# A fused attention and retention layer: keys and values summed in two parts of the model axis, with the sums of the first part kept in DRAM

## The chip, the cores and the metric

The kernel runs on one core of one Trainium2 chip. The metric is device time in microseconds (us) from start to end of one execution. Three runs of the kernel before took 2622.92, 2627.49 and 2629.21 us; the median is 2627.49 us.

## The reference: what is computed

One layer of a diffusion backbone in 32-bit floats: 256 latent tokens and 256 context tokens, model width 4096.

```python
mod = silu(c) @ ada_w + ada_b                   # 4096 x 12288: shift, scale, gate
shift, scale, gate = split(mod, 3)
mod_c = silu(c_ctx) @ ada_w[:, :2*D] + ada_b[:2*D]
h  = rms_norm(x, norm_w) * (1 + scale) + shift
hc = rms_norm(ctx, norm_w) * (1 + scale_c) + shift_c
proj = h @ w_in                                 # 4096 x 14336: q, k, v, gate of both groups
pc   = hc @ w_in[:, keys and values]            # context rows need keys and values only
o_d = diff_attention(...)                       # group A: 8 heads, two softmax maps each
o_r = retention forward + backward              # group B: 8 heads
y = concat(o_d * silu(dg), o_r * silu(rg)) @ w_out   # 4096 x 4096
out = x + gate * y
```

The model axis (4096) is the axis that the projections sum over; it falls into 32 k-tiles of 128. No k-tile of `h` exists before the shift and scale of its 128 columns, and each of these columns is a sum over all 4096 rows of `ada_w`.

## The kernel before, in words

**Exact products.** Every weight k-tile is split into two parts that one pass of the array carries exactly: ScalarE casts the high part (`whi`, L337), VectorE subtracts to get the low part (`wlo`, L338). `h` is held as `hh` and `hl` in SBUF for the whole kernel. One product is three matmuls (hh by hi, hh by lo, hl by hi; L351 to L353, in the startup L489 to L491). A unit is two k-tiles of one head's weights: 512 columns for a head of group A, 384 for one of group B. Keys and values (kv) have four row tiles, latent and context, so a kv unit has 24 matmuls; queries and gate (qg) have two row tiles, so 12. A unit's weights come by SP's queue into `raw` (three buffers); `whi` and `wlo` have four buffers each, which is two units.

**Startup.** `CHUNKS` cuts the model axis into two chunks of one k-tile and fifteen of two. For each chunk the adaLN columns come first: `Ada.unit` (L238) multiplies loaded k-tiles of `ada_w` by the two columns of `c` and `c_ctx` on TensorE, four k-tiles at once in the four column groups of the array (tile `pa`, L253), four loads per call for a chunk of two k-tiles. At the end of a chunk `finish` transposes the sums by small matmuls (`pm`, L268) and VectorE and ScalarE modulate the chunk's k-tiles of `h` in place (L272 to L286). Then the kv units of five heads of group A (A0 to A4) run over the chunk. Heads A0 to A3 take one PSUM bank at a time and add into SBUF on VectorE (`kvqgA`, L497); A4 stays in four banks (`psP`) through the whole startup. `ada_to` places the adaLN bursts among these units, 0.3 of a chunk ahead (`LEAD`).

**Steady state.** `SCHED` orders qg of A0 to A7, kv of A5 to A7, and kv and qg of group B, each over all 32 k-tiles with the sums in PSUM. Between units run steps of the attention of a finished head (`attA`, L614, and `attB`, L722) and, in the kv phases from A6 on, one step of `gate_task` (L804): it loads two k-tiles of the gate columns (`graw`, 512 KB, one load ahead) and VectorE multiplies and adds them into `gacc` (L827, two per step, 128 steps in all). The big SBUF pool `a4` has nine buffers of 4 KB per partition for kv and qg of heads, `graw`, `gacc` and others.

**Output.** The heads' outputs go through DRAM (`o_dram`) and the output projection (`psO`) follows.

The order on each engine is not the program's text: the builder schedules the whole program once against its own estimate of durations, an instruction that is ready going ahead of one that is not, and writes a fixed order for every engine. On the chip each engine works through its order and waits where an operand is late.

Of the kernel before, what the change touches and what calls it, by code (L numbers as in the profile page):

```python
# [10 lines left out]
F32 = mybir.dt.float32  # L11
# [25 lines left out]
CHUNKS = [1, 1] + [2] * 15  # L37
LEAD = 0.3
NS = 5
ADAB = 5  # L40
RAWB = 3

SCHED = ["qg A0", "qg A1", "keep", "kv A5", "qg A2", "qg A3", "gate", "kv A6", "qg A4", "kv A7", "qg A5", "kv B0", "qg A6",
         "kv B1", "qg A7", "kv B2", "attB", "qg B0", "kv B3", "qg B1", "kv B4", "qg B2", "kv B5", "qg B3", "kv B6", "qg B4",
         "kv B7", "qg B5", "qg B6"]
# [27 lines left out]
def hybrid_kernel(es, tc, x, c, ctx, c_ctx, norm_w, ada_w, ada_b, w_in, q_norm_w, k_norm_w,  # L73
# [19 lines left out]

    def aux_tile(shape, name):
        return aux.tile(shape, F32, name=name, tag="aux")
# [5 lines left out]
    tab = cpool.tile([P, C_END], F32, name="tab")  # L101
    nc.scalar.dma_start(tab[:, 0:C_J], ctab[:, 0:C_J])
    ident = tab[:, C_ID:C_ID + P]
    J = tab[:, C_J:C_J + 384]
    cosp = tab[:, C_COS:C_COS + 256].rearrange("p (r d) -> p r d", r=2)
    sinp = tab[:, C_SIN:C_SIN + 256].rearrange("p (r d) -> p r d", r=2)
# [5 lines left out]
    subln = cpool.tile([P, DV], F32, name="subln")  # L112
    retnw = cpool.tile([P, DV], F32, name="retnw")
# [90 lines left out]
    c0s = [sum(CHUNKS[:j]) for j in range(len(CHUNKS))]  # L204
# [6 lines left out]
    ada_end = [sum(1 for a in ada_units if a[0] <= j) for j in range(len(CHUNKS))]  # L211

    class Ada:
# [5 lines left out]
        def load(self):  # L219
            """start the loads of the next unit"""  # L220
# [4 lines left out]
            n = CHUNKS[j] * P  # L225
            c0 = c0s[j] * P
            tiles = []
            # shift and scale columns side by side
            m = 4 // CHUNKS[j]
# [770 lines left out]
```

## Time and profile before

| | before |
|---|---|
| median of 3 runs | 2627.49 us |
| span of the profiled execution | 2625.2 us |
| granted TensorE clock, mean | 0.995 |
| PE busy | 2563.4 us (98%) |
| PEld (weight load) busy | 2114.3 us (81%) |
| VectorE busy | 1550.8 us (59%) |
| ScalarE busy | 990.8 us (38%) |
| read from HBM, written | 523.49 MB, 8.40 MB |

The result does not hold a time of its own for the profiled execution; its span is 2625.2 us, from the first to the last instruction, and it lies among the three runs. The startup lasts from the first projection matmul at 50.0 us to the last one at 680.6 us, the steady state to 2251.3 us, and the output projection to the end. Matmuls are pipelined, so a row's duration (0.40 us for 512 columns) is longer than the distance from one start to the next (0.23 us); a busy PE with fewer instructions per stretch is a slower PE.

### The profile page before, as it was taken

To read this page: it belongs to the slowest core of one execution; us is meant where nothing else is said; L and a number is where in the kernel's file an instruction comes from. 1 tells how busy PE (TensorE), PEld (TensorE's weight loads), DVE (VectorE), ACT (ScalarE), POOL (GpSimd) and SP (SyncE) were. 2 spreads that over 40 slices of the span, in tenths; PEclk is the share of its full clock that TensorE was granted. 3 is DMA by queue.
4 is the path that set the end of the run, shared out by engine and by line. 5 is a ranking of instruction groups with operands and counts; after the bars stand their busy time and mean duration, and the time that the engine had idled before them with its cause. 6 is when DMAs were issued, how large, how long until landed. Compare 5 with 4: busy or idle time off the path is not lost.

```text
span 2625.2 us, 36854 instructions
## 1 busy us (share of the span) xinstructions
PE 2563.4 (98%) x12970; PEld 2114.3 (81%) x12970; DVE 1550.8 (59%) x2898; ACT 990.8 (38%) x1993; POOL 47.3 (2%) x49
## 2 busy tenths in 40 slices
PE   7899999999999999999999999999999999999999
PEld 5466666666778888787989899999999999878887
DVE  6555555555665465756666666657564446755554
ACT  5222222222454453434334433343343445544443
POOL 0000000000000000000000000000000000000000
PEclk8999999999999999999999999999999999999999
DMA  9989988987542453746474757656562546776765
GB/s 308 317 268 291 289 288 276 295 282 222 151 153 93 142 168 120 233 138 211 144 228 150 225 155 208 201 169 219 172 214 89 145 125 189 221 231 206 224 212 173
DMA packets 510521, 534.38 MB, mean 204 GB/s; under 512 B 30640, under 2 KB 433392, under 8 KB 510336
## 3 DMA queue, kind: packets, MB, share of 16 engines
q1 hardware_dynamic: 498176, 511.85, 62.9%
q10 hardware_dynamic: 12160, 20.17, 2.3%
q8 instruction: 103, 1.69, 0.3%
q14 instruction: 82, 0.67, 0.1%
HBM read 523.49 MB, written 8.40 MB: 203 GB/s over the span
## 4 chain that ended last, share of the span: by engine, by line
PE 81%; DMA 11%; DVE 5%; issue 1%; ACT 1%; SPq 1%; POOL 0%; ACTq 0%; DVEq 0%; POOLq 0%
PE psA L352 7%; PE psA L353 7%; PE psA L351 7%; PE psB L352 7%; PE psB L353 7%; PE psB L351 7%; DMA graw<-in_ada_w_dram 6%; PE psO L351 4%; PE psO L352 4%; PE psO L353 4%; PE pa L253 4%; DVE gacc L827 2%; DMA ada<-in_ada_w_dram 2%; PE psA3s L489 1%; PE psA2s L489 1%; PE psA1s L489 1%
## 5 line engine op out<-in xcount | busy, mean ns | idle before, releaser
L352 PE MATMUL psB<-wloB,hh 128*128 128x384 f32 x1536 | 520.8, 339 | 9.4 <-DVE wloB L338 9.3
L353 PE MATMUL psB<-whiB,hl 128*128 128x384 f32 x1536 | 518.0, 337 | 0.0
L351 PE MATMUL psB<-whiB,hh 128*128 128x384 f32 x1536 | 472.3, 338 | 2.0 <-ACT whiB L337 2.0
L338 DVE TENSOR_TENSOR wloB<-rawB,whiB 128x384 fp32r<-128x384 f32 x512 | 280.9, 555 | 242.8 <-ACT whiB L337 241.1
L337 ACT CAST whiB<-rawB 128x384 fp32r<-128x384 f32 x512 | 258.1, 512 | 434.7 <-PE psB L353 371.3
L352 PE MATMUL psA<-wloA,hh 128*128 128x512 f32 x896 | 358.0, 400 | 6.0 <-DVE wloA L338 6.0
L353 PE MATMUL psA<-whiA,hl 128*128 128x512 f32 x896 | 356.1, 397 | 0.0
L338 DVE TENSOR_TENSOR wloA<-rawA,whiA 128x512 fp32r<-128x512 f32 x352 | 241.4, 690 | 193.1 <-ACT whiA L337 191.8
L337 ACT CAST whiA<-rawA 128x512 fp32r<-128x512 f32 x352 | 216.2, 620 | 299.3 <-PE psA L353 251.3
L351 PE MATMUL psA<-whiA,hh 128*128 128x512 f32 x896 | 315.7, 399 | 0.2 <-ACT kvqgA L408 0.2
L352 PEld LDWEIGHTS psB<-wloB,hh 128*128 128x128 f32 x1536 | 289.5, 188 | 16.1 <-DVE wloB L338 14.5
L353 PEld LDWEIGHTS psB<-whiB,hl 128*128 128x128 f32 x1536 | 289.4, 188 | 0.3
L351 PEld LDWEIGHTS psB<-whiB,hh 128*128 128x128 f32 x1536 | 284.5, 188 | 4.4 <-ACT whiB L337 2.6
L338 DVE TENSOR_TENSOR wloO<-rawO,whiO 128x512 fp32r<-128x512 f32 x256 | 175.9, 691 | 150.7 <-ACT whiO L337 150.4
L337 ACT CAST whiO<-rawO 128x512 fp32r<-128x512 f32 x256 | 157.7, 620 | 194.8 <-PE psO L353 165.1
L827 DVE SCALAR_TENSOR_TENSOR gacc<-graw,cT,gacc 128x512 f32<-128x512 f32 x248 | 185.6, 748 | 69.8 <-DMA graw<-in_ada_w_dram 68.2
L352 PEld LDWEIGHTS psA<-wloA,hh 128*128 128x128 f32 x896 | 169.0, 189 | 48.4 <-DVE wloA L338 9.5
L352 PE MATMUL psO<-wloO,ohh 128*128 128x512 f32 x512 | 203.9, 398 | 0.0
L353 PE MATMUL psO<-whiO,ohl 128*128 128x512 f32 x512 | 202.8, 396 | 0.0
L351 PEld LDWEIGHTS psA<-whiA,hh 128*128 128x128 f32 x896 | 168.7, 189 | 40.8 <-ACT kvqgA L408 0.6
L353 PEld LDWEIGHTS psA<-whiA,hl 128*128 128x128 f32 x896 | 169.1, 189 | 39.3
L351 PE MATMUL psO<-whiO,ohh 128*128 128x512 f32 x512 | 162.1, 397 | 1.1 <-ACT whiO L337 0.9
(313 smaller groups left out, 3244.2 us busy)
## 6 DMA issues: line engine op xcount, KB each, us to landing
ada<-in_ada_w_dram SPq DMA_DIRECT2D x512, 256.0 KB
rawA<-in_w_in_dram SPq DMA_DIRECT2D x352, 256.0 KB
graw<-in_ada_w_dram SPq DMA_DIRECT2D x128, 512.0 KB
rawB<-in_w_in_dram SPq DMA_DIRECT2D x256, 256.0 KB
rawO<-in_w_out_dram SPq DMA_DIRECT2D x128, 512.0 KB
rawB<-in_w_in_dram SPq DMA_DIRECT2D x256, 128.0 KB
rawA0s<-in_w_in_dram SPq DMA_DIRECT2D x30, 256.0 KB
rawA1s<-in_w_in_dram SPq DMA_DIRECT2D x30, 256.0 KB
```

What stands on the lines that cost most here:

```text
L253: m = nc.tensor.matmul(self.pa[32 * g:32 * (g + 1), :], cpad[:, 2 * kt:2 * kt + 32], tiles[k], start=(kt < 4), stop=(kt >= KT - 4), tile_p ...
L337: nc.scalar.copy(hi, raw[:, k])
L338: nc.vector.tensor_tensor(lo, raw[:, k], hi.bitcast(F32), op=ALU.subtract)
L351: nc.tensor.matmul(pt[:, :ncol], a, hi, start=f, stop=False)
L352: nc.tensor.matmul(pt[:, :ncol], a, lo, start=False, stop=False)
L353: nc.tensor.matmul(pt[:, :ncol], b, hi, start=False, stop=e)
L489: nc.tensor.matmul(pt, a, hi, start=f, stop=False)
L827: nc.vector.scalar_tensor_tensor(acc, raw[:, k], cT[:, 0, kt:kt + 1], acc, op0=ALU.mult, op1=ALU.add)
```

## The change

The model axis is cut at k-tile 20 (`K1`). The startup now covers k-tiles 0 to 19 alone: two chunks of one and nine of two, with the same five heads. Its adaLN calls take eight k-tiles each, so the bursts on TensorE have eight products (`ADAB`, the buffers for `ada_w`, goes from 5 to 6). At its end the sums of the five heads' keys and values are stored to `p_dram` in DRAM. Then a new phase runs over `FIRST`, the kv units of A5 to A7 and B0 to B7, also over k-tiles 0 to 19; each head's four banks are copied by ScalarE and stored by ScalarE's queue. Between these units `ada2_task` makes the shift and scale of the last 12 k-tiles, in three chunks of four, on VectorE: per k-tile of the sum axis one 512 KB load and two multiply-adds of 128x1024 into two accumulators, then 16 small matmuls against a column of ones per chunk, and the same modulation. The steady state then runs kv over k-tiles 20 to 31 and qg over all 32 for one head after the other; at the third of the six kv units the stored sums are loaded by SP's queue, and VectorE adds PSUM to them. The gate takes two steps per unit in kv of group A and one in kv of group B. The constants of the heads move to a pool that opens when the adaLN pool closes.

```diff
+K1 = 20
+CHUNKS = [1, 1] + [2] * 9
+CHUNKS2 = [4, 4, 4]
-ADAB = 5
+ADAB = 6
+FIRST = [f"A{h}" for h in range(NS, 8)] + [f"B{h}" for h in range(8)]
+SCHED = []
+for _h in range(8):
+    SCHED += [f"kv A{_h}", f"qg A{_h}"]
+SCHED += ["kv B0", "attB", "qg B0"]
...
-        nk = 8 // cn
+        nk = 8
...
+    def ada2_task():
+        work = [(j, k) for j in range(len(CHUNKS2)) for k in range(KT)]
...
+        for i, (j, k) in enumerate(work):
...
+            if k == 0:
+                acc = [a4.tile([P, 2 * n], F32, name=f"acc{j}_{v}", tag="a4") for v in range(2)]
+            for v in range(2):
+                cv = cT[:, v, k:k + 1]
+                if k == 0:
+                    nc.vector.tensor_scalar(acc[v], w, cv, None, op0=ALU.mult)
+                else:
+                    nc.vector.scalar_tensor_tensor(acc[v], w, cv, acc[v], op0=ALU.mult, op1=ALU.add)
+            load()
+            if k == KT - 1:
+                yield
+                pm = aux_tile([P, cn, 4], f"pm2_{j}")
...
+                modulate(c0s2[j], cn, pm)
+            yield
...
+        def before():
+            for i in range(2):
+                hd.dst(2 * i, 0)
+                nc.sync.dma_start(hd.t[i], p_dram[hd.name, i])
...
+                if part:
+                    nc.scalar.copy(d, bank.t[rt][:, :hd.ncol])
+                elif rest:
+                    nc.vector.tensor_tensor(d, bank.t[rt][:, :hd.ncol], d, op=ALU.add)
...
+    def store_part(hd):
+        for i in range(2):
+            nc.scalar.dma_start(p_dram[hd.name, i], hd.t[i])
+            hd.t[i] = None
...
+    for nm in FIRST:
+        run_units(head_units(heads[nm], 0, pairs(0, K1), part=True), between1)
...
+        gate_rate[0] = 0 if kind == "qg" else 2 if hd.kind == "A" else 1
+        if kind == "qg":
+            run_units(head_units(hd, 1, pairs(0, KT)), between)
+        else:
+            run_units(head_units(hd, 0, pairs(K1, KT), rest=True), between)
```

TensorE in the startup, one adaLN burst of a chunk of two k-tiles. Before, it has two k-tile pairs (the number in `ada_26` is the first k-tile of a loaded pair; each product is two records) between the matmuls of heads A2 and A3:

```order
L491 MATMUL psA2s_3_1504<-whiA2s_0_1409,hl_99 128x512
L489 MATMUL psA2s_3_1504<-whiA2s_1_1413,hh_98 128x512
L490 MATMUL psA2s_3_1504<-wloA2s_1_1414,hh_98 128x512
L491 MATMUL psA2s_3_1504<-whiA2s_1_1413,hl_99 128x512
L253 MATMUL pa_1310<-ada_26_1403,cpad 32x512 x2
L253 MATMUL pa_1310<-ada_24_1400,cpad 32x512 x2
L489 MATMUL psA3s_0_1533<-whiA3s_0_1462,hh_98 128x512
```

In the changed program the burst has four pairs, and the projection matmuls between this burst and the next are 18, then 24, 30 and 48 in the course of a chunk:

```order
L557 MATMUL psP_511<-whiA4s_1_2823,hl_133 128x512
L264 MATMUL pa_2940<-ada_6_2707,cpad 32x512 x2
L264 MATMUL pa_2940<-ada_4_2704,cpad 32x512 x2
L264 MATMUL pa_2940<-ada_2_2701,cpad 32x512 x2
L264 MATMUL pa_2940<-ada_0_2698,cpad 32x512 x2
L555 MATMUL psA0s_0_2972<-whiA0s_0_2908,hh_132 128x512
L556 MATMUL psA0s_0_2972<-wloA0s_0_2909,hh_132 128x512
```

The number of bursts per chunk falls from eight to four, each with twice the products.

VectorE in the kernel before, in the kv phase of a group B head with gate steps: among the low parts of the weights (`wloB_0_20_0`: kv, k-tile 20, first of the unit) stand multiply-adds of 128x512 and steps of an attention:

```order
L338 TENSOR_TENSOR wloB_0_18_1_11124<-rawB_0_18_11116,whiB_0_18_1_11123 128x384
L827 SCALAR_TENSOR_TENSOR gacc_10790<-graw_1_10788,cT,gacc_10790 128x512 x2
L338 TENSOR_TENSOR wloB_0_20_0_11159<-rawB_0_20_11155,whiB_0_20_0_11158 128x384
L666 TENSOR_REDUCE stA_10921<-scA_11090 128x1
L666 TENSOR_REDUCE stA_10922<-scA_11094 128x1
L827 SCALAR_TENSOR_TENSOR gacc_10790<-graw_2_10835,cT,gacc_10790 128x512
L667 SCALAR_TENSOR_TENSOR stA_10921<-stA_10921,qsA_10728 128x1
L667 SCALAR_TENSOR_TENSOR stA_10922<-stA_10922,qsA_10728 128x1
L827 SCALAR_TENSOR_TENSOR gacc_10790<-graw_2_10835,cT,gacc_10790 128x512
L338 TENSOR_TENSOR wloB_0_20_1_11163<-rawB_0_20_11155,whiB_0_20_1_11162 128x384
```

VectorE in the changed program, first part of head B3: among the low parts stand the multiply-adds of 128x1024 of the new task (`acc_0` for `c`, `acc_1` for `c_ctx`; the last number of `ada_2_3` is the k-tile of the sum axis):

```order
L327 SCALAR_TENSOR_TENSOR acc_0_6619<-ada_2_2_6414,cT,acc_0_6619 128x1024
L391 TENSOR_TENSOR wloB_0_4_0_6341<-rawB_0_4_6337,whiB_0_4_0_6340 128x384
L327 SCALAR_TENSOR_TENSOR acc_1_6620<-ada_2_2_6414,cT,acc_1_6620 128x1024
L391 TENSOR_TENSOR wloB_0_4_1_6345<-rawB_0_4_6337,whiB_0_4_1_6344 128x384
L327 SCALAR_TENSOR_TENSOR acc_0_6619<-ada_2_3_6454,cT,acc_0_6619 128x1024
L391 TENSOR_TENSOR wloB_0_6_0_6381<-rawB_0_6_6377,whiB_0_6_0_6380 128x384
L327 SCALAR_TENSOR_TENSOR acc_1_6620<-ada_2_3_6454,cT,acc_1_6620 128x1024
L327 SCALAR_TENSOR_TENSOR acc_0_6619<-ada_2_4_6494,cT,acc_0_6619 128x1024
L391 TENSOR_TENSOR wloB_0_6_1_6385<-rawB_0_6_6377,whiB_0_6_1_6384 128x384
L327 SCALAR_TENSOR_TENSOR acc_1_6620<-ada_2_4_6494,cT,acc_1_6620 128x1024
L391 TENSOR_TENSOR wloB_0_8_0_6421<-rawB_0_8_6417,whiB_0_8_0_6420 128x384
```

From the first low part of a head to that of the next there are 20 low parts and, for A5, A6, A7, B0 to B7 in turn, 31, 33, 0, 26, 20, 18, 27, 19, 18, 0 and 0 multiply-adds or their opening products.

VectorE in the changed program, second part of head A1 with the attention of A0: the gate's multiply-adds stand four to a unit, as far as the attention's steps leave room:

```order
L937 SCALAR_TENSOR_TENSOR gacc_8489<-graw_13_9150,cT,gacc_8489 128x512
L391 TENSOR_TENSOR wloA_0_24_1_9162<-rawA_0_24_9154,whiA_0_24_1_9161 128x512
L701 TENSOR_TENSOR t1A0k<-kvqgA_0_8546,tab_8372 128x4x32 x4
L937 SCALAR_TENSOR_TENSOR gacc_8489<-graw_13_9150,cT,gacc_8489 128x512
L391 TENSOR_TENSOR wloA_0_26_0_9209<-rawA_0_26_9205,whiA_0_26_0_9208 128x512
L704 TENSOR_TENSOR kvqgA_0_8546<-kvqgA_0_8546,tab_8372 128x2x256
L937 SCALAR_TENSOR_TENSOR gacc_8489<-graw_14_9197,cT,gacc_8489 128x512
L391 TENSOR_TENSOR wloA_0_26_1_9213<-rawA_0_26_9205,whiA_0_26_1_9212 128x512
L705 TENSOR_TENSOR kvqgA_0_8546<-kvqgA_0_8546,t1A0k 128x2x256
L937 SCALAR_TENSOR_TENSOR gacc_8489<-graw_14_9197,cT,gacc_8489 128x512
```

In this order 13 to 18 of a head's 24 gate instructions stand in its kv units, the others among its qg units.

## Rows read from the trace of the kernel before

**Rows 1.** The profile's page, busy time of each engine (us, share of the span, instructions).

```profile
PE 2563.4 (98%) x12970; PEld 2114.3 (81%) x12970; DVE 1550.8 (59%) x2898; ACT 990.8 (38%) x1993; POOL 47.3 (2%) x49
```

**Rows 2.** Windows by stage; columns: stretch and length, busy us per engine, clock, DMA share, GB/s.

```profile
50.00:146.20 96.20, 89.23 (x452) 52.22 (x452) 52.83 (x93) 23.76 (x43) 0.00 (x0) 0.97 0.95 299
146.20:680.90 534.70, 527.20 (x2605) 339.00 (x2602) 301.70 (x558) 122.18 (x225) 2.91 (x1) 1.00 0.84 267
680.90:2251.30 1570.40, 1548.88 (x8108) 1404.60 (x8107) 958.04 (x1850) 648.06 (x1387) 39.74 (x36) 1.00 0.56 171
2251.30:2619.60 368.30, 367.19 (x1591) 294.96 (x1590) 205.30 (x325) 164.30 (x276) 2.20 (x4) 1.00 0.67 210
```

**Rows 3.** Timeline of PE in the startup; columns: start us, duration us, line, tiles, count.

```profile
325.43 0.39 PE L491 MATMUL psA2s<-whiA2s,hl 128*128 128x512 f32 x1
325.75 1.07 PE L253 MATMUL pa<-ada,cpad 128*32 128x512 f32 x8
326.74 0.50 PE L489 MATMUL psA3s<-whiA3s,hh 128*128 128x512 f32 x1
327.08 0.40 PE L490 MATMUL psA3s<-wloA3s,hh 128*128 128x512 f32 x1
327.31 0.40 PE L491 MATMUL psA3s<-whiA3s,hl 128*128 128x512 f32 x1
...
336.71 0.39 PE L491 MATMUL psP<-whiA4s,hl 128*128 128x512 f32 x1
336.94 0.95 PE L268 MATMUL pm<-tab,ms 128*128 128x2 f32 x8
337.82 1.07 PE L253 MATMUL pa<-ada,cpad 128*32 128x512 f32 x8
```

**Rows 4.** Timeline of the weight loads, two bursts side by side in the startup.

```profile
300.06 0.19 PEld L491 LDWEIGHTS psP<-whiA4s,hl 128*128 128x128 f32 x1
300.62 0.16 PEld L253 LDWEIGHTS pa<-ada,cpad 128*32 128x32 f32 x8 [0.37 <-DVE hl L285]
...
302.47 0.53 PEld L489 LDWEIGHTS psA0s<-whiA0s,hh 128*128 128x128 f32 x3 [0.84 <-issue]
303.05 0.19 PEld L490 LDWEIGHTS psA0s<-wloA0s,hh 128*128 128x128 f32 x1
```

**Rows 5.** Windows, one stretch of the startup.

```profile
65.00:130.00 65.00, 58.05 (x286) 31.80 (x285) 34.17 (x60) 12.97 (x24) 0.00 (x0) 0.97 0.99 318
```

**Rows 6.** Groups by form, VectorE; columns: tiles and shapes, count, busy us, mean ns, idle before.

```profile
L338 DVE TENSOR_TENSOR wloB<-rawB,whiB 128x384 fp32r<-128x384 f32 x512 | 280.9, 555 | 242.8 <-ACT whiB L337 241.1 <-issue 0.6
L338 DVE TENSOR_TENSOR wloA<-rawA,whiA 128x512 fp32r<-128x512 f32 x352 | 241.4, 690 | 193.1 <-ACT whiA L337 191.8
L827 DVE SCALAR_TENSOR_TENSOR gacc<-graw,cT,gacc 128x512 f32<-128x512 f32 x248 | 185.6, 748 | 69.8 <-DMA graw<-in_ada_w_dram 68.2
L302 DVE SCALAR_TENSOR_TENSOR junk<-x 128x1024 f32<-128x1024 f32 x4 | 4.9, 1215 | 0.9 <-DMA x<-in_ctx_dram 0.9
```

**Rows 7.** Timeline of VectorE in a stretch with gate steps.

```profile
1585.20 0.75 DVE L827 SCALAR_TENSOR_TENSOR gacc<-graw,cT,gacc 128x512 f32<-128x512 f32 x1 [1.40 <-DMA graw<-in_ada_w_dram]
1585.87 0.68 DVE L600 TENSOR_TENSOR aTA<-aTpA,aTA 128x512 fp32r<-128x512 f32 x1
1586.47 0.74 DVE L827 SCALAR_TENSOR_TENSOR gacc<-graw,cT,gacc 128x512 f32<-128x512 f32 x1
...
1597.01 0.75 DVE L827 SCALAR_TENSOR_TENSOR gacc<-graw,cT,gacc 128x512 f32<-128x512 f32 x1 [2.18 <-DMA graw<-in_ada_w_dram]
```

**Rows 8.** Timeline of SP's queue, the load that the last of these waits for.

```profile
1591.54 2.04 SPq L808 DMA_DIRECT2D graw<-in_ada_w_dram  x1
```

**Rows 9.** Windows, a stretch of group B's projections without gate steps, and one with.

```profile
1285.00:1325.00 40.00, 40.00 (x233) 39.34 (x232) 26.27 (x51) 14.41 (x32) 0.00 (x0) 1.00 0.56 173
1300.00:1365.00 65.00, 61.80 (x329) 56.50 (x329) 48.49 (x88) 24.89 (x61) 1.53 (x2) 0.97 0.69 217
```

**Rows 10.** Waits; columns: who waits for whom, us in total, times, longest.

```profile
DVE gacc L827 <- DMA graw<-in_ada_w_dram: 68.2, 69, 3.2
```

More of the change, by code (lines that the diff above doesn't have):

```diff
@@ L92, in hybrid_kernel @@
     g_dram = dram.tile([1, D], F32, name="g_dram")
+    p_dram = {}
+    for k in "AB":
+        for h in range(8):
+            for i in range(2):
+                p_dram[f"{k}{h}", i] = dram.tile([P, 2, 512 if k == "A" else 384], F32, name=f"p_dram{k}{h}_{i}")
     def aux_tile(shape, name):
@@ L247, in unit @@
             prev = None
-            for k0 in range(0, nk, 4):
-                for k in (k0 + 3, k0 + 2, k0 + 1, k0):
-                    g, kt = k % 4, u0 + k
-                    with nullcontext() if prev is None else tc.issue_after(prev):
-                        m = nc.tensor.matmul(self.pa[32 * g:32 * (g + 1), :], cpad[:, 2 * kt:2 * kt + 32], tiles[k],
-                                             start=(kt < 4), stop=(kt >= KT - 4), tile_position=None)
-                    prev = m.ins if hasattr(m, "ins") else m
+            for i, k in enumerate(range(nk - 1, -1, -1)):
+                g, kt = k % 4, u0 + k
+                with nullcontext() if prev is None else tc.issue_after(prev):
+                    m = nc.tensor.matmul(self.pa[32 * g:32 * (g + 1), :], cpad[:, 2 * kt:2 * kt + 32], tiles[k],
+                                         start=(u0 == 0 and i < 4), stop=(u0 + nk == KT and i >= nk - 4),
+                                         tile_position=None)
+                prev = m.ins if hasattr(m, "ins") else m
             if self.pos == ada_end[j]:
@@ L361, in hybrid_kernel, with __init__ @@
     class Unit:
-        def __init__(self, segs, kt0, nk, ps_get, name, first, last, nrt, w_ap=None, xs=None, after=None):
+        def __init__(self, segs, kt0, nk, ps_get, name, first, last, nrt, w_ap=None, xs=None, after=None, before=None):
             self.__dict__.update(locals())
@@ L372, in run @@
             self.prepare()
+            if self.before is not None:
+                self.before()
             ncol = sum(s[1] for s in self.segs)
@@ L434, in after @@
                 d = hd.dst(rt, qg)
-                if first_acc:
+                if part:
[3 more added lines that the diff above has]
+                else:
                     evict(d, bank.t[rt][:, :hd.ncol])
-                else:
-                    nc.vector.tensor_tensor(d, bank.t[rt][:, :hd.ncol], d, op=ALU.add)
+            if part:
+                store_part(hd)
         for i, (kt0, nk) in enumerate(ktseq):
             last = i == len(ktseq) - 1
-            units.append(Unit(segs[qg], kt0, nk, bank, f"{hd.name}{tag}_{qg}_{kt0}", i == 0, last, nrt,
-                              after=after if last else None))
+            units.append(Unit(segs[qg], kt0, nk, bank, f"{hd.name}_{qg}_{kt0}", i == 0, last, nrt,
+                              after=after if last else None,
+                              before=before if rest and i == max(0, len(ktseq) - 4) else None))
         return units
@@ L487, in run @@
                     f = k == 0 if not keep else kt == 0
-                    e = k == nk - 1 if not keep else kt == KT - 1
+                    e = k == nk - 1 if not keep else kt == K1 - 1
                     nc.tensor.matmul(pt, a, hi, start=f, stop=False)
@@ L972, in hybrid_kernel @@
     atB_cm.__exit__(None, None, None)
+    c2_cm.__exit__(None, None, None)
     hA_cm.__exit__(None, None, None)
```

152 lines of the change are left out of this document (90 added, 62 removed).

## The prediction

> **What bounds the kernel now.** I read the page's busy times first, then windows by stage, then the timeline inside the startup, and last the groups, timeline and waits of VectorE. PE is busy 98% of the span [rows 1], so in nearly every stretch TensorE's own instructions set the pace, and what counts is how many of them there are and how far apart they start. The stages show it [rows 2]: PE is idle 7.5 us of 534.7 in the startup from 146 us on, 21.5 us of 1570.4 in the steady state and 1.1 us in the output stage. The clock is at 1.00 in these stages, the upper level of 2.4 GHz, and the change gives PE no long pause in which it could fall. In the output stage 1591 instructions take 368.3 us, 0.2315 us for a matmul of 512 columns; the startup's plain matmuls start 0.23 us apart too [rows 3]. A matmul of 384 columns takes 40.00 / 233 = 0.172 us [rows 9].
>
> In the startup PE does other things than projections. A burst of adaLN products sits between the start at 325.43 and that at 327.08, 1.65 us with two plain matmuls in it, so it costs 1.65 - 0.46 = 1.19 us; the eight `pm` records cost 1.11 - 0.23 = 0.88 us [rows 3]. A chunk of two k-tiles has eight bursts and one `pm` group: 8 x 1.19 + 0.88 = 10.4 us beside 120 x 0.2315 = 27.8 us of projections. VectorE is busy 302 of 534.7 us there, and DMA at a share of 0.84 with 267 GB/s [rows 2], while one stretch moved 318 GB/s [rows 5].
>
> **The change, part by part.** The sum is made against the profiled span, 2625.2 us; the median of the runs, 2627.49 us, is 2.3 us above it, and I add these at the end.
>
> (a) Six chunks leave the startup. Their projections are done later at the same 0.23 us, so what goes is 6 x 10.4 = 62 us. From the other side: 50.0 to 680.9 us is 630.9 us, of which 1920 x 0.2315 = 444 us are projections; 12/32 of the rest is 70 us, but this holds the slow start. I take 65 us off.
>
> (b) Bursts of eight in the nine remaining chunks. The trace has two bursts side by side once: from the load at 300.06 to that at 303.05 are 2.99 us, with four plain distances of 0.23 in them, so 2.06 us against 2 x 1.19 = 2.38, and 0.3 us is saved per merged pair [rows 4]. Of 36 merged pairs nine are side by side already: 27 x 0.3 = 8 us. Against it stands DMA. A chunk moves 8.4 MB of `ada_w` and 2.6 MB of weights, 11.0 MB; in 27.8 + 4 x 2.06 + 0.9 = 36.9 us that is 298 GB/s, between the 267 of the stage and the 318 of the best stretch. Only 18 matmuls (4.2 us) lie between the first and second burst of a chunk, and the second half of the second burst's loads can start only when the first burst frees its buffers: 1 MB, 3.3 us at 318 GB/s and some start and landing time. I take -4 us, and keep -8 and +21 (11.0 MB at 267 GB/s is 41.2 us a chunk, 2.3 above the present 38.9, times nine) as ends.
>
> (c) New small matmuls: three chunks of 16 against a column of ones, two records each. Eight records cost 0.88 us, so 3 x 32 / 8 x 0.88 = 11 us on PE. Nothing hides them; if their latency is shared better, 6 us.
>
> (d) The first part for A5 to B7. VectorE gets 192 operations of 128x1024. The nearest row is 1.215 us [rows 6]. Starts on VectorE are 0.67 us apart where the row says 0.75, and 0.60 where it says 0.68 [rows 7], so one takes 0.08 us less than its row: 1.135, and a low part 0.475 (B) or 0.61 (A). Per head PE needs 240 x 0.172 = 41.2 us (B) or 55.6 us (A). A6, with most multiply-adds, needs 20 x 0.61 + 33 x 1.135 = 50 us on VectorE; B3 20 x 0.475 + 27 x 1.135 = 40 and some 2 us of modulation; B0 the same with 26 and 3 us. So VectorE and PE are level in B0 and B3, and VectorE has slack in the others. Behind a multiply-add on VectorE are queued the low parts that PE waits for, and PE holds two units of 4.1 us at most. I take +10 us, with ends 0 and +28: the whole durations make B0 and B3 5 us late each, and the eight heads with multiply-adds (358 us of PE) could each lose at the rate of a dense stretch of before, 3.2 us in 65 [rows 9], 18 us.
>
> Here a rule speaks against the change. The Trainium skill, VectorE: DVE Perf Modes, The DRAIN you can't avoid, says that the next VectorE operation does not start until the pipe of the one before is empty. This trace's starts lie 0.08 us ahead of the reported ends [rows 7]; by the rule every operation costs its full row, and the sum would be some 8 us higher.
>
> (e) The changeover. Ten stores of 512 KB go out on ScalarE's queue, the first eight behind the last VectorE adds, and behind them on ScalarE wait the casts of the next units; four banks of A4 have to be copied before A5 has its third and fourth bank. PE has a unit of 5.6 us in hand. I take +4, ends 0 and +12.
>
> (f) The steady state. The gate's 128 steps now fall mostly on kv of group A, two per unit. Per A head VectorE has 44 low parts (26.8 us), 24 gate operations (16 us), four additions of the stored sums (2.4 us), and attention and the like: of the stage's 958 us [rows 2] the three large groups [rows 6] make 708, which leaves 250 us for 15 heads, 17 us each. That is 62 us beside 336 x 0.2315 = 77.8 us of PE: 80%. The dense stretch before had 75% and lost 3.2 us of 65 [rows 9], by waits for `graw`, which sum to 68 us on VectorE [rows 10]; the last of [rows 7] waits 2.18 us for a load whose issue began 5.5 us earlier [rows 8]. Eight A heads of some 85 us with attention at that rate are 33 us; the B heads have few gate steps left, 4 us. Before, the stage lost 21.5 us in all. So +16 us, ends -15 (the waits vanish, as VectorE's other work covers the loads) and +60 (the rival below).
>
> At nothing I put: the 14.7 MB stored and loaded again (11 GB/s over the span, hidden beside PE; were each reload to hold up SP's queue by 2 us, 32 us); VectorE alone adding the four banks at the end of kv, because the qg units need only two banks, which are free (else 16 x 1.2 us); the heads' constants, behind the units of B6 and B7, which have no multiply-adds (else 10 us once).
>
> Sum: -65 - 4 + 11 + 10 + 4 + 16 = -28; 2625.2 - 28 = 2597, and with the 2.3 us of the median 2600 us.
>
> **The rivals.**
>
> R1, slower: the gate's loads bind kv of group A. Two steps per unit want two 512 KB loads of 5.5 us in 5.6 us of PE, and `a4` has room for two or three `graw`; kv weights, `graw` and the reloads ask 10.4 MB in 37 us, 280 GB/s. If four waits of 2.2 us per A head come through to PE, as the longest of [rows 7] did, that is 70 us in place of 16: 2654. It decides from about 9 us of PE idle per A head on. For it: the waits exist with one step per unit already. Against it: PE lost 21.5 us in the stage although VectorE waited 68, and a third to a half of the gate's operations stands among the qg units.
>
> R2, no change: DMA binds the startup. Chunks of 41.2 us, (b) at +21: 2600 + 25 = 2625. For it: the DMA share of 0.84 to 0.95; against it: 318 GB/s for 65 us.
>
> R3: VectorE binds the first part, at +28, by full durations and late loads: 2618.
>
> R4, more: the bursts pay in full (-8), first part and changeover are free and the steady state gets rid of most gate waits (-10): 2625.2 - 65 - 8 + 11 - 10 + 2.3 = 2556. For it: average load of VectorE stays below 70%.
>
> By the rule of the Trainium skill in (d) (VectorE: DVE Perf Modes, The DRAIN you can't avoid) the forecast would move to 2608; the starts of [rows 7] are against it.
>
> **How the numbers follow.** Forecast 0.46 (its own range 2583 to 2617), R1 0.13, R2 0.13, R3 0.14, R4 0.14. A measurement of this kernel can tell 0.3% from no change, 7.9 us: faster is below 2619.6, slower above 2635.4. Faster: 0.45 of the forecast, 0.14 of R4, 0.08 of R3 and 0.04 of R2, together 0.71. Slower: most of R1 and a little of R2, 0.14. The same: 0.15. The range leaves out half of R4's spread below and the upper half of R1 above: 2564 to 2640.
>
> **What would show it.** Right: the startup's last matmul near 450 us, chunks of 37 to 39 us; the first part of about 500 us with PE idle under 15 us; PE idle in the steady part near 35 us. (a) is wrong if the startup ends after 470 us; (b) if PE waits for `ada` at the second burst of a chunk by more than 2 us; (d) if `wloB` holds PE in B0 and B3 by more than 5 us each, or in the other heads at all; (f) if `graw` waits on VectorE exceed 100 us or kv of an A head takes more than 46 us. The forecast as a whole falls if the stretch from the startup's end to the output stage grows by more than PE's moved matmuls and 45 us.

## The result, and the profile after

The changed kernel takes 2548.97 us (median of 4 runs, 2548.26 to 2552.09), against 2625.2 us of the kernel before in the runs made with it: a ratio of 0.9709, 95% interval 0.9694 to 0.9723. The forecast was 2600 us with a range from 2564 to 2640. The sign was right, and the gain is 2.8 times the one forecast (76 us against 27). The profiled run has a span of 2547.1 us, 78.1 less than before. Two single executions below, one of 10392.47 us in experiment 12 and one of 3060.35 us of the changed kernel beside it, are in the slow state and are left out of all comparisons.

The page's busy times after, to be put beside [rows 1] (PE is TensorE's matmuls, PEld its weight loads, DVE VectorE, ACT ScalarE):

```profile
PE 2496.5 (98%) x12634; PEld 2125.9 (83%) x12634; DVE 1718.8 (67%) x3028; ACT 1000.9 (39%) x2011; POOL 46.3 (2%) x49
```

PE is as full as before, of less work; VectorE has 168 us more. The same windows by stage as in [rows 2], with the columns as there; the first part of A5 to B7 is a new second stage, and the steady state is the third:

```profile
50.00:442.20 392.20, 373.50 (x1889) 254.62 (x1886) 218.94 (x386) 89.42 (x161) 0.00 (x0) 0.99 0.89 284
442.20:955.80 513.60, 513.60 (x2737) 480.52 (x2735) 378.21 (x507) 149.98 (x289) 2.91 (x1) 1.00 0.65 206
956.00:2169.40 1213.40, 1207.42 (x6191) 1070.86 (x6191) 885.69 (x1747) 564.99 (x1230) 39.89 (x38) 1.00 0.67 208
```

The balance, with the projections that change their stage taken at before's distances from one matmul's start to the next (720 x 0.2335 us for k-tiles 20 to 31 of A0 to A4, and 720 x 0.2335 + 1920 x 0.172 = 498.3 us for the first part):

| stage | before | after | moved projections | rest | forecast of the rest |
|---|---|---|---|---|---|
| startup from 50.0 us | 630.9 | 392.2 | -168.1 | -70.6 | -69, (a) and (b) |
| first part | - | 513.8 | +498.3 | +15.5 | +25, (c), (d), (e) |
| steady state | 1570.4 | 1213.4 | -330.2 | -26.8 | +16, (f) |
| output, to the end | 373.9 | 377.7 | 0 | +3.8 | 0 |

The rest sums to -78.1. With the median distances of the trace before, 0.234 and 0.173 us, the first part's rest is 13 and the steady state's -25, so 2 us can move between these rows. 43 us of the 50 us between forecast and result lie in one row, the steady state, 9.5 in the first part. PE's idle time in the steady state was 21.5 us before [rows 2]; it is 6.0 now, where 35 was forecast. Over the eight A heads, where the forecast had 33 us of loss, VectorE is busy 526 of 692 us, 76%, and PE is idle for 2.1 us:

```profile
956.00:1648.10 692.10, 689.98 (x3116) 558.26 (x3116) 525.73 (x991) 316.75 (x695) 27.20 (x21) 1.00 0.70 223
```

VectorE waited for the gate's loads before [rows 10] and does so still, with a total that is only a little lower, 60 us (second row: the first operation of a column block):

```profile
DVE gacc L937 <- DMA graw<-in_ada_w_dram: 49.7, 30, 4.1
DVE gacc L935 <- DMA graw<-in_ada_w_dram: 10.1, 3, 4.0
```

Where such waits reach PE is seen in the groups of PE that read the low parts (`wlo`); the last column is PE's idle time before them and who ended it. Before:

```profile
L352 PE MATMUL psB<-wloB,hh 128*128 128x384 f32 x1536 | 520.8, 339 | 9.4 <-DVE wloB L338 9.3
L352 PE MATMUL psA<-wloA,hh 128*128 128x512 f32 x896 | 358.0, 400 | 6.0 <-DVE wloA L338 6.0
```

After:

```profile
L405 PE MATMUL psA<-wloA,hh 128*128 128x512 f32 x896 | 357.6, 399 | 2.1 <-DVE wloA L391 2.1
L405 PE MATMUL psB<-wloB,hh 128*128 128x384 f32 x896 | 303.7, 339 | 2.2 <-DVE wloB L391 2.2
```

15.3 us of waits for low parts have become 4.3. The reason shows when a load's issue on SP's queue is put beside the gate's operations on VectorE. Before, SP's queue in kv of B0 (start, duration, line, tiles, count):

```profile
1305.09 0.37 SPq L808 DMA_DIRECT2D graw<-in_ada_w_dram  x1
...
1307.00 4.21 SPq L808 DMA_DIRECT2D graw<-in_ada_w_dram  x2
...
1313.69 0.37 SPq L808 DMA_DIRECT2D graw<-in_ada_w_dram  x1
```

And VectorE there:

```profile
1304.31 0.75 DVE L827 SCALAR_TENSOR_TENSOR gacc<-graw,cT,gacc 128x512 f32<-128x512 f32 x1
...
1305.45 1.53 DVE L827 SCALAR_TENSOR_TENSOR gacc<-graw,cT,gacc 128x512 f32<-128x512 f32 x2
...
1309.27 0.75 DVE L827 SCALAR_TENSOR_TENSOR gacc<-graw,cT,gacc 128x512 f32<-128x512 f32 x1 [0.43 <-DMA graw<-in_ada_w_dram]
...
1312.91 0.75 DVE L827 SCALAR_TENSOR_TENSOR gacc<-graw,cT,gacc 128x512 f32<-128x512 f32 x1
```

Gate operations end at 1305.06, 1306.98 and 1313.66, and 0.02 to 0.03 us after each a load is issued: it had waited for the buffer that the operation gave back. The first of these loads is used 4.2 us later, and VectorE waits 0.43 us for it, with low parts queued behind. After, in kv of A1, SP issues four at once as the head begins:

```profile
1036.53 2.01 SPq L918 DMA_DIRECT2D graw<-in_ada_w_dram  x4
...
1049.90 0.37 SPq L918 DMA_DIRECT2D graw<-in_ada_w_dram  x1
```

From issue to first use, the lead of a load, the median of the 128 loads is 5.0 us before and 7.4 after (issues on SP's timeline paired with the uses on VectorE's). A load is called under way from its issue to the end of its last use; the number under way at an issue, itself included, is two or fewer for 88 loads before and for 50 after.

### The profile page after: what moved, and what is told of

The parts are those of the page before. It is cut to its first block, busy times and chain, and to the rows that moved or that the text cites. A ratio compares the mean times of both kernels' runs of the same rounds, so it can differ in the third digit from the quotient of the medians.

```text
span 2547.1 us, 36352 instructions
## 1 busy us (share of the span) xinstructions
PE 2496.5 (98%) x12634; PEld 2125.9 (83%) x12634; DVE 1718.8 (67%) x3028; ACT 1000.9 (39%) x2011; POOL 46.3 (2%) x49
## 4 chain that ended last, share of the span: by engine, by line
PE 90%; DMA 6%; DVE 2%; SPq 1%; issue 1%; ACT 1%; DVEq 0%; POOL 0%; ACTq 0%; POOLq 0%
PE psA L405 8%; PE psA L406 8%; PE psA L404 8%; PE psB L405 6%; PE psB L406 6%; PE psB L404 6%; PE psO L404 5%; PE psO L405 5%; PE psO L406 5%; DMA ada<-in_ada_w_dram 3%; PE pa L264 3%; DMA graw<-in_ada_w_dram 1%; PE psA3s L555 1%; PE psA1s L555 1%; PE psP L556 1%; PE psP L555 1%
## 5 line engine op out<-in xcount | busy, mean ns | idle before, releaser
L390 ACT CAST whiA<-rawA 128x512 fp32r<-128x512 f32 x412 | 253.9, 620 | 425.0 <-PE psA L406 242.0
L391 DVE TENSOR_TENSOR wloA<-rawA,whiA 128x512 fp32r<-128x512 f32 x412 | 281.8, 687 | 152.3 <-ACT whiA L390 147.9
L405 PE MATMUL psB<-wloB,hh 128*128 128x384 f32 x896 | 303.7, 339 | 2.2 <-DVE wloB L391 2.2
L406 PE MATMUL psB<-whiB,hl 128*128 128x384 f32 x896 | 302.4, 337 | 0.0
L404 PE MATMUL psB<-whiB,hh 128*128 128x384 f32 x896 | 263.9, 339 | 1.2 <-ACT whiB L390 1.2
L327 DVE SCALAR_TENSOR_TENSOR acc<-ada,cT,acc 128x1024 f32<-128x1024 f32 x186 | 233.8, 1277 | 0.0
L405 PEld LDWEIGHTS psB<-wloB,hh 128*128 128x128 f32 x896 | 169.0, 189 | 4.4 <-DVE wloB L391 3.7
L406 PEld LDWEIGHTS psB<-whiB,hl 128*128 128x128 f32 x896 | 168.9, 189 | 0.3
```

The costliest lines, as they stand in the source:

```text
L327: nc.vector.scalar_tensor_tensor(acc[v], w, cv, acc[v], op0=ALU.mult, op1=ALU.add)
L390: nc.scalar.copy(hi, raw[:, k])
L391: nc.vector.tensor_tensor(lo, raw[:, k], hi.bitcast(F32), op=ALU.subtract)
L404: nc.tensor.matmul(pt[:, :ncol], a, hi, start=f, stop=False)
L405: nc.tensor.matmul(pt[:, :ncol], a, lo, start=False, stop=False)
L406: nc.tensor.matmul(pt[:, :ncol], b, hi, start=False, stop=e)
```

## The experiments

Theory G: PE lost its time in the steady state of the kernel before where low parts stand behind gate steps on VectorE. Rival O: the order of projections and attention does it, whatever the gate. From experiment 5 on G has a sharper form, L: what counts is how many gate loads can be under way, so how many buffers of `a4` are free for them. Its rival S: the changed order leaves VectorE slack enough, whatever the room. "The stage" is the steady state, 1570.4 us before and 1213.4 in the changed kernel; five more traces with its steady state untouched (the repeat in 12, the three of 7 and that of 10) have it at 1213.3 to 1216.1 us.

**1. The kernel before without the gate's multiply-adds.**

```
-                    nc.vector.scalar_tensor_tensor(acc, raw[:, k], ..., acc, ...)
```

> The kernel before, with the gate's multiply-adds left out (all but the first of each column block, so the gate is wrong); its loads stay. Theory G (in the steady state of the kernel before, PE lost its time where low parts stand behind gate steps on VectorE): the stage from the startup's end to the output stage, 1570.4 us, falls by 13 to 20 us, and PE's waits for low parts, 15.3 us, fall below 6. Theory O (the losses come from the order of heads and attention, the gate is only the one that shows up as the releaser): less than 5 us.

Measured: 2600.47 us, ratio 0.9882 (0.9867 to 0.9897); the stage 1541.0 us, 29.4 less; PE's waits for low parts of A and B are zero. G holds, and by more than expected.

**2. The kernel before, the gate from one resident load.**

```
-            if v + 1 < n:
-                nxt = load(v + 1)
```

> The kernel before, with all of the gate's multiply-adds reading one load that stays (so the gate is wrong, and 127 of its 128 loads of 512 KB are gone); VectorE's work is the same. If the loss came from waiting for the gate's loads, the stage falls by 13 to 20 us as without multiply-adds; if it came from VectorE's work itself, it falls by less than 5 us and the waits for low parts stay at 12 us or more.

Measured: 2601.7 us, ratio 0.9882 (0.9866 to 0.9899); the stage 1544.9 us, 25.5 less, though VectorE is as busy as ever (1559.0 us against 1550.8). Its groups on PE:

```profile
L352 PE MATMUL psB<-wloB,hh 128*128 128x384 f32 x1536 | 519.1, 338 | 0.0
...
L352 PE MATMUL psA<-wloA,hh 128*128 128x512 f32 x896 | 356.7, 398 | 0.0
```

So waiting for loads cost 25 us and the work itself some 4. The edit takes 127 of the 128 loads off the DMA engines as well; that this traffic was not the cause shows in experiment 1, where the loads stay and the time falls too. The loss that I read as 21.5 us, and put down to how busy VectorE is, was almost wholly this.

**3. The changed kernel, gate steps moved into group B.**

```
-        gate_rate[0] = 0 if kind == "qg" else 2 if hd.kind == "A" else 1
+        gate_rate[0] = 1 if hd.kind == "B" or (kind == "kv" and hd.h >= 4) else 0
+        gate_half[0] = kind == "qg"
```

> The changed kernel, with the gate's steps moved from kv of group A (two per unit) to the density of the kernel before, one per 4 us of PE, in group B: 24 steps in kv of A4 to A7, 48 in kv of B, 56 in qg of B. Theory G: PE's losses come back, the stage of 1214.6 us becomes 1228 to 1245 us and the whole 2562 to 2580. Theory O: within 5 us of the changed kernel, 2544 to 2554.

In qg every second unit has a step. Measured: 2563.7 us, ratio 0.9745 (0.9731 to 0.976), in G's range; stage 1225.3 us, just under G's 1228; PE waits 8.2 us for `wloB`. The place of the steps is worth 12 us of the stage. The qg phases of B take 328.8 us in all against 312.5 in the changed kernel, the kv phases of A 275.2 against 281.1. The lead is long here (median 7.7 us), which speaks against the buffers. A likely reason is that in qg of B, PE has 12 matmuls to a unit and not 24, and so uses up low parts twice as fast; no run shows it.

**4. The changed kernel in before's order, qg after the next head's kv.**

```
-    SCHED += [f"kv A{_h}", f"qg A{_h}"]
+    SCHED += [f"kv A{_h}", f"qg A{_h - 1}"]
```

> The changed kernel with the kernel before's order of heads: qg of a head comes after kv of the next one, so that its attention lies beside other units; the gate as in the changed kernel. Theory O: most of the 25 us by which the stage beat the old rate is lost, 2562 to 2575 us. Theory G: within 5 us of the changed kernel, 2544 to 2554.

Measured: 2589.52 us, ratio 0.9844 (0.983 to 0.9859), stage 1255.7 us, 42 more. By the expectations this speaks for O, and the loss is larger than O had it. But the trace has VectorE's waits for `graw` at more than twice those of the changed kernel, and a median lead of 5.7 us; of 128 loads 60 were issued with no other under way (15 in the changed kernel):

```profile
DVE gacc L936 <- DMA graw<-in_ada_w_dram: 121.9, 71, 3.9
DVE gacc L934 <- DMA graw<-in_ada_w_dram: 5.0, 1, 5.0
```

By the program's order two heads' kv and qg then stand in `a4`. PE waits 12.5 us for `wloA`, and 17.2 us in two waits for `gah`, the high part of a finished column block of the gate, whose small matmul (`pg`) PE's fixed order has ahead of further projections:

```profile
PE pg L944 <- ACT gah L708: 17.2, 2, 9.1
```

The changed kernel has no such wait. Order and room come together here; the next runs separate them.

**5. That order, with one more buffer for the gate while group A runs.** Every third load has a buffer of its own.

```
+            own = gpopen[0] and v % 3 == 0
-            raw = a4.tile([P, 2, 512], ...)
+            raw = (gpool if own else a4).tile([P, 2, 512], ...)
```

> The lagged order (qg of a head after kv of the next), with one more buffer for the gate while group A runs: every third load has a buffer of its own outside a4. Theory L (the lagged order lost 40 us since two heads' kv and qg stay in a4 and leave the gate two buffers): 10 to 25 us of the 40 come back, 2565 to 2580 us, and the waits of PE for low parts of A, 12.5 us, fall below 6. Rival A (the lagged order loses by where attention and additions fall): 2584 to 2594 us.

Measured: 2557.93 us, ratio 0.9746 (0.9724 to 0.9769), stage 1226.0: 30 of the 42 us come back by one buffer (26 by the ratios), more than the 10 to 25 expected. The expectation on PE's idle time misses (waits for `wloA` only fall from 12.5 to 9.8, below 6 was expected); what goes is the wait for `gah`, from 17.2 us to none. The 12.6 us that are left to the changed kernel may be the order of heads, or room that is still short: 87 loads have at most one other under way, 50 in the changed kernel.

**6. The kernel before, with the same buffer.** The edit is that of 5.

> The kernel before with one more buffer for the gate's loads while group A runs (every third load has one of its own outside a4, until about 1560 us). Theory L2: the stalls between matmuls of 1040 to 1560 us, 11 us, fall to 4 or less, the whole 4 to 8 us below the kernel before; the later ones, 13 us after 1560, stay. Rival: the stalls stay, within 2 us.

Measured: 2612.09 us, ratio 0.9936 (0.9921 to 0.995), stage 1552.5 us. Longer gaps between matmuls of the projections (over 0.05 us above the usual distance): from 1040 to 1625 us 17.8 us before and 2.9 here, after that, where the buffer is gone, 14.3 and 13.6. (At 1625 us no gate step runs: before, none stands between 1606 and 1669 us, here none between 1590 and 1653.) The groups on PE:

```profile
L352 PE MATMUL psB<-wloB,hh 128*128 128x384 f32 x1536 | 519.8, 338 | 5.4 <-DVE wloB L338 5.4
...
L352 PE MATMUL psA<-wloA,hh 128*128 128x512 f32 x896 | 356.5, 398 | 0.0
```

One buffer of 4 KB per partition, for part of the stage, is worth 16 us to the kernel before; 4 to 8 were expected.

**7. Buffers held, which held nothing.** One, two and four tiles of `a4` were taken ahead of the gate and used once more behind it:

```
+    parked = [a4.tile([P, 8], F32, name=f"park{i}", tag="a4") for i in range(1)]
     ...
+        nc.vector.tensor_scalar(pk, pk, 1.0, None, op0=ALU.add)
```

> The changed kernel with one of the nine 4 KB buffers of a4 held from the start of the steady state until the gate is done, so that one less is free for the gate's loads. Theory L (the number of free buffers sets how early a gate load is issued, and so whether VectorE waits for it in front of low parts): the time between issue and first use falls from a median of 7.4 us towards 6, VectorE's waits for graw rise from 49.7 to 70 to 100 us, and the whole comes to 2554 to 2566 us. Rival S (the even order of heads leaves VectorE enough slack, whatever the lead): 2545 to 2553 us.

> The same with two buffers held, about the room that the kernel before had for the gate's loads. Theory L: the lead falls to the 5.0 us of the kernel before, waits for graw over 110 us, the whole 2570 to 2610 us. Rival S: 2545 to 2555 us.

> The changed kernel with four of the nine buffers of a4 held during the gate, after two were held without any effect. Theory L2 (what counts is whether the load for step v+2 can be issued before step v is used; the changed kernel has at least two buffers more than that): with four held it falls below, leads fall to 4 to 5 us, waits for graw exceed 90 us, the whole 2570 to 2600 us. Rival S (buffers play no part in the order of the changed kernel): 2546 to 2555 us.

Measured: 2551.2, 2549.67 and 2547.84 us. The closing operation depends on nothing of the gate, and ran right behind the opening one, at 962.7 us with one tile, ahead of the gate's first operation, so the buffers were free again; the number of loads under way is that of the changed kernel. The runs say nothing on L; they show how far repeats differ.

**8. Buffers held until the gate's last sum.**

```
+                if v == n - 1:
+                    for pk in parked:
+                        nc.vector.tensor_tensor(pk, acc[:, 0:8], pk, op=ALU.add)
```

> The changed kernel with one of the nine buffers of a4 really held while the gate runs (its last use reads the gate's last sum; in the runs with 'held' buffers before, the closing operation depended on nothing, stood ahead of the gate, and nothing was held). Theory L2 (what decides is how many gate loads can be under way): fewer loads three deep, the median from issue to use falls from 7.4 to 5.5 to 7 us, the whole 2550 to 2565 us. Rival S (the even order of heads does it, whatever the room): 2545 to 2553 us.

> The same with two buffers really held, the least the kernel can run with. Theory L2: one or two loads under way as in the lagged order, leads of 4 to 5.5 us, waits for graw of 100 us and more, the whole 2570 to 2600 us. Rival S: 2545 to 2555 us.

Measured: one held 2556.8 us, ratio 0.9727 (0.9708 to 0.9747); two held 2600.7 us, 0.9898 (0.988 to 0.9916). Stages 1222.4 and 1261.8 us, median leads 6.0 and 5.4 us, VectorE's waits for `graw` 84 and 137 us. With two held, the order of heads unchanged:

```profile
DVE gacc L937 <- DMA graw<-in_ada_w_dram: 131.9, 77, 4.8
DVE gacc L935 <- DMA graw<-in_ada_w_dram: 5.0, 1, 5.0
```

and on PE

```profile
L405 PE MATMUL psA<-wloA,hh 128*128 128x512 f32 x896 | 361.8, 404 | 12.4 <-DVE wloA L391 12.3
...
L405 PE MATMUL psB<-wloB,hh 128*128 128x384 f32 x896 | 303.9, 339 | 7.2 <-DVE wloB L391 7.1
```

and among PE's waits, with the row of PE's timeline for the longer of the two:

```profile
PE pg L948 <- ACT gah L709: 16.5, 2, 8.5
```

```profile
1171.50 0.64 PE L948 MATMUL pg<-gah,onesr 128*32 128x512 f32 x1 [8.48 <-ACT gah L709]
```

L holds: two buffers are worth 48 us of the stage, the second alone 39, and S falls. Two kinds of waits of PE make up most of the 48 us. Low parts behind a late gate step hold PE for 19.4 us (4.3 in the changed kernel). And at the end of two of the eight column blocks PE waits 8.5 and 8.0 us for `gah`, the high part of the finished block (none in the changed kernel). VectorE's rows ahead of the longer one show that the block's last loads come one at a time:

```profile
1157.65 1.54 DVE L937 SCALAR_TENSOR_TENSOR gacc<-graw,cT,gacc 128x512 f32<-128x512 f32 x2 [1.10 <-DMA graw<-in_ada_w_dram]
1163.02 0.75 DVE L937 SCALAR_TENSOR_TENSOR gacc<-graw,cT,gacc 128x512 f32<-128x512 f32 x1 [3.82 <-DMA graw<-in_ada_w_dram]
...
1169.21 1.54 DVE L937 SCALAR_TENSOR_TENSOR gacc<-graw,cT,gacc 128x512 f32<-128x512 f32 x2 [1.45 <-DMA graw<-in_ada_w_dram]
```

The load used at 1163.02 was issued at 1159.22, 0.03 us after the operations of the first row had ended, and the one used at 1169.21 at 1165.39, 0.03 us after the use of the load before it. So a kernel short of buffers loses not only by low parts. With two held, 62 of the 128 loads are issued with no other under way and 52 with one; that the kernel takes the time that I forecast for the changed one is chance. With one held, 87 loads go as the second of a pair, as 75 do in the kernel before, and only 9 us of the stage are lost. That is one trace, of the slowest of the four runs; the interval of the whole time overlaps that of the changed kernel. The kernel before lost 25. The rest may be the place of the steps beside the longer units of A, as experiment 3 has it; the shares were not measured apart.

**9. The changed kernel without the gate's multiply-adds.** The edit is that of 1.

> The changed kernel with the gate's multiply-adds left out (all but the first of each column block, so the gate is wrong); its loads stay. In the kernel before this took 27 to 30 us off. If the gate no longer costs PE anything in the changed kernel but its few remaining waits (17.7 us of longer gaps between matmuls, 6.0 us of PE idle in the stage), 5 to 10 us go: 2539 to 2544 us; if a further 20 us are still lost to it in small pieces: 2520 to 2530.

Measured: 2546.06 us, ratio 0.969 (0.9672 to 0.9709), stage 1210.2 us, 3.2 less than with them. The gate's operations cost the changed kernel some 3 us, less than the 5 to 10 expected, and cost the kernel before 29.4 (experiment 1): the difference, 26.2, is the -26.8 of the balance within its error of 2 us.

**10. Bursts of four again.**

```
-        nk = 8
+        nk = 8 // cn
```

> The changed kernel with the adaLN products of the startup in bursts of four, as before (two of them per old place in the order). Theory P (PE sets a chunk's period, and two bursts merged save 0.3 us): the startup, 442.2 us, ends 4 to 8 us later, 2553 to 2557 us in all. Rival D (DMA sets a chunk's period, at 284 GB/s): the startup ends within 2 us of 442, the whole at 2546 to 2551.

Measured: 2544.71 us, ratio 0.9683 (0.9667 to 0.97). Two theories were set against each other: P, that PE sets a chunk's period and the long burst saves time, and D, that DMA sets it. Both fall: the startup ends earlier, at 437.0 us, where eleven traces with bursts of eight have 441.6 to 444.6. PE's time in the products and its idle time before them, with bursts of eight

```profile
L264 PE MATMUL pa<-ada,cpad 128*32 128x512 f32 (+1 forms) x704 | 83.2, 582 | 18.4 <-DMA ada<-in_ada_w_dram 18.3
```

and with bursts of four

```profile
L265 PE MATMUL pa<-ada,cpad 128*32 128x512 f32 (+1 forms) x704 | 87.9, 576 | 7.9 <-DMA ada<-in_ada_w_dram 7.7
```

The long burst saves 4.7 us of product time and waits 10.5 us more for loads, which it needs all at once.

**11. 16 and 18 k-tiles in the first part.**

```
-K1 = 20
-CHUNKS = [1, 1] + [2] * 9
-CHUNKS2 = [4, 4, 4]
+K1 = 16
+CHUNKS = [1, 1] + [2] * 7
+CHUNKS2 = [4, 4, 4, 4]
```

> The changed kernel with 16 k-tiles in the first part and 16 on VectorE (four chunks of four). The startup should end two chunks, 77 us, earlier, of which 56 us are projections that come back later. Theory V (VectorE was level with PE in the first part): 256 multiply-adds of 1.28 us, 90 us of low parts and 20 us of modulation are 437 us against PE's 399 us and 13 us of small matmuls, so the first part takes 435 to 450 us and the whole 2545 to 2562 us. Rival W (starts 0.08 us early and a greedy fill leave a margin): first part 412 to 422 us, the whole 2525 to 2538 us.

> The changed kernel with 18 k-tiles in the first part and 14 on VectorE (chunks of 4, 4, 4 and 2). One chunk less in the startup is 38.7 us less with 28 us of projections moved, so -10.7; with 16 k-tiles PE's stalls in the first part were 31 us, with 20 2.5. Theory V (a threshold: VectorE's work fills PE's time at about 19 k-tiles): 224 multiply-adds in 456 us of PE give 5 to 12 us of stalls, the whole 2545 to 2551 us. Rival: stalls under 4 us, 2537 to 2543 us.

Measured: with 16, 2555.47 us, ratio 0.974 (0.9718 to 0.9761); with 18, 2546.31 us, 0.9683 (0.9669 to 0.9697). The first part takes 431.0, 467 and 513.8 us for 16, 18 and 20 k-tiles; over the projections that is 32.4, 18.5 and 15.5 us, of which 14.8, 13.0 and 11.1 us are the small matmuls (11.1 us for 12 k-tiles, the others in proportion). So the rest, which is what VectorE and the changeover cost PE, is 17.6, 5.5 and 4.4 us. V, that VectorE's work fills PE's time, holds for both whole times; the first part with 16, 431 us, lies between V's 435 at least and W's 422 at most. With 16, VectorE is late above all in B5. Window over the first part, and B5's group:

```profile
366.70:797.70 431.00, 416.61 (x2209) 389.20 (x2207) 406.80 (x492) 123.73 (x243) 3.82 (x1) 0.98 0.79 256
```

```profile
L405 PE MATMUL psB5p<-wloB,hh 128*128 128x384 f32 x64 | 23.6, 368 | 12.9 <-DVE wloB L391 12.9
```

**12. 18 k-tiles and bursts of four together.**

> 18 k-tiles in the first part and bursts of four: two steps that gained 2 to 5 us each in their own runs, where the startup's bursts of four waited 3.6 us for adaLN loads in place of 14.0. If they add up: startup's end at 400 us (405.1 with bursts of eight), the whole 2536 to 2543 us. If the chunk's period is DMA's alone with the loads one chunk shorter: no gain over either, 2543 to 2549 us.

> 18 k-tiles and bursts of four once more, beside the changed kernel on the same chip, since its first runs spread from 2538 us upwards and their median, 2546.3, and the profiled span, 2536.2, do not agree. If the two steps add up: 2536 to 2542 us, 6 us or more below the changed kernel; if not: 2543 to 2548 us.

> The changed kernel itself, for the comparison on one chip: 2545 to 2553 us.

Measured: the first time 2544.9 us and a ratio of 0.9681 (0.9661 to 0.97), too wide to tell. The second time 2542.53 us, 0.9667 (0.9653 to 0.9682), beside the changed kernel's 2549.9 us, 0.97 (0.9686 to 0.9713), on the same chip: some 7 us or 0.3% faster than the changed kernel, with intervals that don't meet. The startup ends at 398.5 us. That the two steps add up is not shown: either alone has 0.9683, and the intervals overlap. This version has the lowest median.

## Why the prediction was wrong

**(f), the step that failed: +16 forecast, -26.8 measured.** It scaled before's loss by how busy VectorE is, 80% against 75%, and took the room for loads as it was ("`a4` has room for two or three `graw`", R1). Both halves were wrong. The loss was not one of VectorE's work: with the work but without the loads it was gone (experiment 2), and the A heads of the changed kernel, with VectorE at 76%, lose 2.1 us where 33 were forecast. And the room was no constant: by the program's order qg now follows its own head's kv, so one head instead of two keeps its tiles in `a4`, and of the gate's loads most often three are under way (63 of 128) where there were two (75 of 128); with two buffers held and the order kept, 48 us are lost (experiment 8). The trace could have told. The issue of [rows 8] lasts 2.04 us, to 1593.58, and the operations ahead of it on VectorE, in the gap of [rows 7], end at 1593.57:

```profile
1590.46 3.11 DVE L827 SCALAR_TENSOR_TENSOR gacc<-graw,cT,gacc 128x512 f32<-128x512 f32 x4
```

An issue that ends as the operation ends that used the buffer had waited for it. I counted the 5.5 us to the use from its start, and took them for the DMA's; from its end they are 3.4. The lower end of (f), -15, was named for "the waits vanish", but with another condition (that VectorE's other work covers the loads; more loads under way is what the runs show), and was still too small: in experiment 1, 29.4 us went with the gate, against 21.5 of PE's idle time in all. The difference is likely lower clock and gaps too small for the idle column; it was not split. The signs named for (f) being wrong looked the other way only: VectorE's waits for `graw` stayed at 60 us, under 100, and kv of an A head takes 35 us, under 46. R4 (2556 us) had the right direction and came nearest.

**(a), right in sign, and (b), wrong.** Together -69 forecast, -70.6 measured; the agreement is partly luck. With bursts of four the startup's rest is 387.0 - 630.9 + 168.1 = -75.8 us: (a) was too small by some 10 us (this holds the sixth buffer for `ada`, which was not tried alone), and (b) is +5 and not -4. I had the right reason against it, the loads of the second burst, and took the other side. What was to show (b) wrong, a wait of more than 2 us for `ada` at the second burst of a chunk, is there in one chunk, 2.7 us; from 146 us on the second bursts wait 0.6 to 1.7 us.

**(c) as forecast**: 96 records of 11.1 us in all.

**(d) and (e): +14 forecast, 4.4 measured** (2 with the median distances). From their first matmul to the end of their last, B0, B3 and B6 take 45.7, 46.8 and 45.3 us against 41.8 of B7, and of this 3.2 to 3.7 us is the `pm` group. In the window 610.8 to 652.4 us of B0 VectorE is busy 41.18 of 41.6 us; starts are 1.20 us apart where the row has 1.28:

```profile
611.78 1.28 DVE L327 SCALAR_TENSOR_TENSOR acc<-ada,cT,acc 128x1024 f32<-128x1024 f32 x1
612.98 0.55 DVE L391 TENSOR_TENSOR wloB<-rawB,whiB 128x384 fp32r<-128x384 f32 x1
613.44 1.28 DVE L327 SCALAR_TENSOR_TENSOR acc<-ada,cT,acc 128x1024 f32<-128x1024 f32 x1
```

The 186 three-operand multiply-adds last 1.277 us (233.8 us in all), 0.06 more than the row that I took, and not one waited: VectorE was level, as said, but PE was never idle in the first part (513.60 of 513.60 us); that the two units in hand at PE absorbed it is likely and was not measured. The margin ends between 18 and 16 k-tiles (experiment 11). The rule weighed at (d) is qualified in the Trainium skill itself: Perfetto Trace Analysis, DVE / Act Engine Instruction, has the reported end at the acknowledgement of the write and lets the next operation begin to fetch its data once the one before has finished executing. The 0.08 us by which starts lie ahead of reported ends here agree with that.

**The output stage**, at nothing, is 3.8 us longer; PE waits 3.9 us there for `ohh`, 0.2 before. It wasn't pursued; a second trace of the changed kernel has 375.1 us there against 377.7, so most of it is within what repeats differ by.

The rivals: R1's waits come when two buffers are held (experiment 8); R2's time for a chunk, 41.2 us, did not come (36 to 39 us from 110 us on, with 284 GB/s in the stage), though its mechanism, late loads at the second burst, did, by 10 us; R3's binding begins beyond the changed kernel's split.

## What to carry to other kernels

When load after load is issued, or its issue ends, just as the operation ends that used a buffer (0.01 to 0.03 us here), the wait behind it is one for room first: count the buffers that an order leaves free before scaling a loss by how busy an engine is. A change that reorders heads changes how long their tiles live, and with it the depth of every other stream in the same pool; one buffer of 4 KB per partition was worth 16 us to one kernel and some 30 to another. A late stream costs time at every place where PE's fixed order depends on it, here behind low parts and at the end of a column block. A test that holds a buffer must close on data that come last.

## What the runs showed of the hardware

Behind some pauses of PE its clock is lower for a while, so that such a pause costs more than its length. In the kernel before, PE waits 2.85 us for `wloA` until 1348.29 us; from 1349.15 to 1352.36 its matmuls of 512 columns are 0.43 us apart, nearly twice the 0.2335. The granted clock is 0.51 there, the lower level, 1.2 GHz. Timeline of PE, and windows with the granted clock in the third column from the right:

```profile
1348.29 0.50 PE L352 MATMUL psA<-wloA,hh 128*128 128x512 f32 x1 [2.85 <-DVE wloA L338]
...
1350.65 0.63 PE L352 MATMUL psA<-wloA,hh 128*128 128x512 f32 x1
1351.07 0.63 PE L353 MATMUL psA<-whiA,hl 128*128 128x512 f32 x1
1351.50 0.63 PE L352 MATMUL psA<-wloA,hh 128*128 128x512 f32 x1
```

```profile
1335.00:1345.00 10.00, 9.69 (x54) 9.09 (x55) 7.11 (x14) 2.31 (x5) 0.98 (x1) 1.00 0.73 239
1349.00:1352.50 3.50, 3.50 (x11) 2.58 (x10) 3.46 (x9) 2.47 (x7) 0.55 (x1) 0.51 0.83 249
```

With two buffers held (experiment 8), the 8.48 us of waiting for `gah` are followed by 5 us like that:

```profile
1171.50:1176.80 5.30, 5.30 (x13) 3.98 (x14) 4.48 (x8) 3.21 (x7) 0.00 (x0) 0.50 0.66 203
```

Summed over neighbouring projection matmuls whose distance is near twice the usual one, the time lost by it is 1.9 us in the steady state before, 1.5 after and 5.0 with two buffers held, where the mean clock of the run is 0.988 against 0.993 of the changed kernel.
